# Tying each DMA of the weight sums to the matmuls of the weight unit in front of it, with descriptors of 4 KB

## The chip, the cores and the metric

The kernel runs on one core of a Trainium2 chip. The metric is the device time of one execution in microseconds. A core has a matrix engine (PE), a vector engine (DVE), an activation engine (ACT), a general engine (POOL, GpSimd) and SyncE (SP), each with its own queue of instructions that it works through in order, and 16 DMA engines that serve the DMAs issued by SP, ACT and POOL alike. Engines wait for one another through semaphores.

## The reference

The reference is the trunk of a streaming encoder: two layers over 512 frames of width 1024, in float32. What matters here is the shape of the work and the hidden layer at the end of a layer:

```python
for i in range(DEPTH):                      # 2 layers
    h = rmsnorm(x, norm1_g[i])
    z = h @ w_in[i] + b_in[i]               # 1024 x 12296: all projections
    ...                                     # branch A: mLSTM, 4 heads; branch B: retention, 4 heads
    merged = sigmoid(gm) * (y_m @ w_bm[i]) + sigmoid(gr) * (y_r @ w_br[i])
    x = x + merged @ w_out[i]
    h2 = rmsnorm(x, norm2_g[i])
    x = x + square(relu(h2 @ w_ff1[i] + b_ff1[i])) @ w_ff2[i] + b_ff2[i]
    h3 = rmsnorm(x, norm3_g[i])
    x = x + sigmoid(h3 @ w_pe_gate[i]) * (p[i] @ w_pe[i])
return rmsnorm(x, final_g)
```

## The kernel before

**Weights.** Every product is made of three matmuls (`mm3`: high part by high part, high by low, low by high), since a float32 operand is split into two parts for PE. The weights come in units of 512 KB from a stream in DRAM. SP loads them into five raw buffers (`fill_raws`, L278); ACT makes the high part (`wh`, L238) and DVE the low part (`wl`, L239) in `split`. There are three buffers of split pieces, and the split runs two pieces ahead of the matmuls (`LOOK`). Most units are a `T8`: 1024 rows by 128 columns, 24 matmuls of 512 columns. A `V` unit is a quarter of a value projection, in `values`, whose matmuls are written there and don't go through `mm3`. `unit(kind)` is called at the start of each such unit, before its matmuls are written; it counts the units.

**The order of a layer** is that of `unit_list`: 187 units. Gates (`IF`, tile names l0if, l1if); the q and k of mLSTM head 0 with a convolution (l0m0z), its values (l0m0vp), two branch gates (l0bgm), then head by head the scores (l0m0s, with a decay tile l0m0D), the product with the values (l0m0a), the output gates (l0m0o) and the transposes back (l0m0ot); then the retention heads (l0r0brq and on), the merge, `w_out`, and the hidden layer (l0f), whose second product is done in `PAIR` units.

**The weight sums.** A `PAIR` works on blocks of `w_ff2` by a scheme of seven products instead of eight. It needs four sums and differences of given blocks, t1 to t4, each 1 MB: t1 = B12 + B11, t3 = B12 + B22, t2 = t1 + B22, t4 = t2 + B21, for each of the four blocks b of a layer: 16 sums a layer. They are made by DMAs alone, DRAM to DRAM, issued on POOL: a copy of the first term into the sum's tensor (L253), then a DMA that adds the second (L256). The add needs the copy landed, and the copy of t1 into t2 needs the add of t1 landed. The tensors are called s00t to s13t in the profile (layer, block). `sum_steps(i)` gives the steps of a layer, 11 for a block: eight DMAs and three that do nothing. `unit` takes the next step at every third unit (`STEP`), counted over both layers. `fill_raws` loads the sums for the `PAIR` units (L276).

**Order on the engines.** A planner orders the instructions of each engine by its own idea of when their inputs are ready. A sum's DMA has no input but given weights and earlier sums. The trace shows what that gave: on POOL the sums of both layers stand in the first 330 us, in the middle of the work of layer 0.

**What else POOL does.** The sums of squares for the norms (L422) and their power (L436), the borders of the convolution's tiles (`conv_evac`, L682), the causal mask of each decay tile (an affine select, L729, in `m_scores`), and the power in the head norms (L750 for the mLSTM, L792 for the retention). The masked decay goes to DVE (L508), which multiplies the scores by it, and then to ACT and DVE (`split` again, tile l0m0ph), both of which also make the weights' parts in the same queues.

Of the kernel before, what the change touches and what calls it, by code (L numbers as in the profile page):

```python
# [35 lines left out]
F32R = mybir.dt.float32r  # L36
AF = mybir.ActivationFunctionType
OP = mybir.AluOpType

P = 128  # L40
T = 512
# [48 lines left out]
MADE = {"t1": ("B12", "B11"), "t3": ("B12", "B22"), "t2": ("t1", "B22"), "t4": ("t2", "B21")}  # L90
# [3 lines left out]
STEP = 3  # L94
# [95 lines left out]
def build(ctx, tc, ins, out):  # L190
    nc = tc.nc
    ve, ac, gp, te = nc.vector, nc.scalar, nc.gpsimd, nc.tensor
# [17 lines left out]
    cur = {}  # L210
# [20 lines left out]
    def ps(name):  # L231
        return psum.tile([P, T], F32, name=name, tag="ps")
# [4 lines left out]
    def split(src, hi_ap, lo_ap):  # L237
        ac.activation(hi_ap, src, AF.Copy)  # L238
        ve.tensor_sub(lo_ap, src, hi_ap.bitcast(F32))  # L239


    sums = {(i, b, x): tc.dram_tile([4, P, Q], F32, name=f"s{i}{b}{x}") for i in range(L) for b in range(4) for x in MADE}

    def block(i, b, x):
        return ins["wpairs"][i, b, GIVEN.index(x)] if x in GIVEN else sums[i, b, x]

    def flat(a):
        return a.rearrange("a p q -> (a p q)").rearrange("(r w) -> r w", r=P)

    def sum_steps(i):  # L250

        def copy(b, x):
            gp.dma_start(flat(block(i, b, x)), flat(block(i, b, MADE[x][0])))  # L253

        def add(b, x):
            gp.dma_start(flat(block(i, b, x)), flat(block(i, b, MADE[x][1])), accum_op=OP.add, max_dma_last_dim=8192)  # L256

        for b in range(4):
            for f, x in ((copy, "t1"), (copy, "t3"), (add, "t1"), (add, "t3"), (copy, "t2"), (None, None), (add, "t2"),
                         (None, None), (copy, "t4"), (None, None), (add, "t4")):  # L260
                yield (lambda f=f, b=b, x=x: f and f(b, x))


    order = [(n, x) for n, u in enumerate(units) for x in (PIECE if u[0] == "PAIR" else (0,))]
# [28 lines left out]
    def ready(k):  # L293
        while at["prep"] < min(len(order), k + 1):
            prep_next()

    def unit(kind):
        n = at["unit"]
        at["unit"] += 1
        if n % STEP == 0:  # L300
            next(cur["steps"], lambda: None)()
        assert units[n][0] == kind, (units[n], kind)
        ready(place[n, 0] + LOOK)
        return units[n], *pieces.pop((n, 0))

    def mm3(o, sh, sl, mh, ml, first, last):
        te.matmul(o, sh, mh, start=first, stop=False)  # L307
        te.matmul(o, sh, ml, start=False, stop=False)  # L308
        te.matmul(o, sl, mh, start=False, stop=last)  # L309

    def t8(act, name):

        _, wh, wl = unit("T8")
        o = ps(name)
        for k in range(KT):
            s = slice(k * P, (k + 1) * P)
            mm3(o, wh[:, s], wl[:, s], act[0][k], act[1][k], k == 0, k == KT - 1)
        return o
# [49 lines left out]
    def pair_operand(name, st, hi, lo):  # L368

        v = st.rearrange("p (q t) -> p q t", t=S)  # L370
        ve.tensor_tensor(v[:, 4:6, :], v[:, 1:3, :], v[:, 0:1, :].to_broadcast([P, 2, S]), OP.subtract)
        ve.scalar_tensor_tensor(v[:, 6, :], v[:, 5, :], -1.0, v[:, 1, :], OP.mult, OP.subtract)
        ve.scalar_tensor_tensor(v[:, 7, :], v[:, 6, :], -1.0, v[:, 3, :], OP.mult, OP.subtract)
        split(st[:, 4 * S:8 * S], hi[:, 3 * S:7 * S], lo[:, 3 * S:7 * S])
# [5 lines left out]
    class Norm:  # L380
# [18 lines left out]
        def operand(self, k, x):  # L399
            hi, lo = self.act[0][k], self.act[1][k]  # L400
            ac.activation(hi, x, AF.Copy, scale=self.col(k))
            ve.scalar_tensor_tensor(lo, x, self.col(k), hi.bitcast(F32), OP.mult, OP.subtract)

        def square(self, k, x, pool=False):
# [6 lines left out]
            if pool:  # L411
                gp.tensor_tensor(sq, x, x, OP.mult)
            else:
# [60 lines left out]
    def values(i, nm, act, nrm, bv_ap, n_):  # L474
        bvt = cur["br"].tile([P, T], F32, name=f"{nm}bv", tag="bv")
        nc.sync.dma_start(bvt, bv_ap)
        o = [ps(f"{nm}vp{j}") for j in range(NT)]
        for u in range(4):
            _, wh, wl = unit("V")
            for kk in range(2):  # L480
                k = 2 * u + kk
                s = slice(kk * T, (kk + 1) * T)
                for j in range(NT):
                    js = slice(j * P, (j + 1) * P)
                    te.matmul(o[j], act[0][k][:, js], wh[:, s], start=(k == 0), stop=False)
                    te.matmul(o[j], act[0][k][:, js], wl[:, s], start=False, stop=False)
                    te.matmul(o[j], act[1][k][:, js], wh[:, s], start=False, stop=(k == KT - 1))
        vh = [cur["low"].tile([P, 576], F32R, name=f"{nm}vh{j}", tag="vh", bufs=NT) for j in range(NT)]
        vl = [cur["low"].tile([P, 576], F32R, name=f"{nm}vl{j}", tag="vl", bufs=NT) for j in range(NT)]
        for j in range(NT):  # L490
            rows_split_v(i, None, nm, n_, j, o[j], nrm.c, bvt, vh[j], vl[j])
        return vh, vl

    def scores(nm, qh, ql, kh, kl, decay):

        ph = cur["br"].tile([P, 1280], F32R, name=f"{nm}ph", tag="ph")
        pl = cur["br"].tile([P, 1280], F32R, name=f"{nm}pl", tag="pl")
        off = 0
        offs = []
        for i in range(NT):  # L500
            w = T - i * P
            c0 = min(i * P, 256)
            o = ps(f"{nm}s{i}")
            s = slice(i * P, (i + 1) * P)
            for d in range(2):
                mm3(o[:, c0:T], kh[d][:, s], kl[d][:, s], qh[d][:, c0:T], ql[d][:, c0:T], d == 0, d == 1)
            p = tmp(f"{nm}p{i}")
            ve.tensor_tensor(p[:, :w], o[:, i * P:T], decay(i), OP.mult)  # L508
            split(p[:, :w], ph[:, off:off + w], pl[:, off:off + w])
            offs.append(off)  # L510
            off += w
        return ph, pl, offs

    def attend(nm, pt, vh, vl, c0, n, num):
        ph, pl, offs = pt
        for j in range(NT):
            o = ps(f"{nm}a{j}")
            for i in range(j + 1):
                s = slice(offs[i] + (j - i) * P, offs[i] + (j - i + 1) * P)
                mm3(o[:, :n], ph[:, s], pl[:, s], vh[i][:, c0:c0 + n], vl[i][:, c0:c0 + n], i == 0, i == j)  # L520
            ac.activation(num[:, j, :], o[:, :n], AF.Copy)
# [99 lines left out]
    x = bpool.tile([P, KT, T], F32, name="x0", tag="big")  # L621
# [15 lines left out]

    for i in range(L):
        cur["steps"] = sum_steps(i)
        act_side, ph_side = ("right", "left") if i == 0 else ("left", "right")  # L640
        xa = n1.act
# [24 lines left out]


        _, wh, wl = unit("IF")
        og = ps(f"l{i}if")
        for k in range(KT):  # L670
# [151 lines left out]
        for d in range(4):  # L822
            o = t8(xa, f"l{i}m0z{d}")
# [39 lines left out]
        for c in range(KT):  # L863
            o = t8(ym, f"l{i}bm{c}")
# [16 lines left out]
        for c in range(KT):  # L881
            o = t8(yr, f"l{i}br0{c}")
# [9 lines left out]
        mh, ml = [], []  # L892
        for c in range(KT):
# [3 lines left out]
            o = t8(yr, f"l{i}br1{c}")  # L897
# [13 lines left out]
        x = bpool.tile([P, KT, T], F32, name=f"l{i}x", tag="big")  # L911
        n2_pool = phase(f"n2{i}", act_side)
        n2 = Norm(f"l{i}n2", i, "g2", acts(n2_pool, f"l{i}n2"))
        for c in range(KT):
            xr = tmp(f"l{i}xr{c}")
            nc.scalar.dma_start(xr[:, :T], x_src[c])
            o = t8((mh, ml), f"l{i}wo{c}")
# [99 lines left out]
        for u in range(2):  # L1017
            _, wh, wl = unit("PE")
            for c in range(4):
                o = ps(f"l{i}pe{u}{c}")  # L1020
# [10 lines left out]
        last = i == L - 1  # L1031
# [21 lines left out]
        for c in range(KT - LAST if last else KT):  # L1053
            o = t8(n3.act, f"l{i}pg{c}")
# [27 lines left out]
    for a, n in enumerate(nn):  # L1082
        for c in range(KT - LAST, KT):
            _, wh, wl = ws[c - KT + LAST]
            o = ps(f"pl{a}{c}")[:, :256]
# [131 lines left out]
```

## Time and profile before

| what | value |
|---|---|
| time, median of 3 runs (lowest to highest) | 2515.81 us (2515.69 to 2518.84) |
| time of the profiled execution | 2519.82 us |
| its span, first to last instruction | 2518.1 us |
| mean granted PE clock | 0.974 |
| PE busy | 2409.3 us, 96% |
| DVE, ACT, POOL busy | 1502.3, 1051.1, 166.1 us |
| moved by DMA | 333.72 MB, of it 67.11 MB by POOL's queue (q0) |

The profile is of one execution. Busy times add up instructions; a waiting engine isn't busy. The page cuts the span into 40 slices of 63 us and gives the busy share of each in tenths. Other views give the busy time in chosen windows, the waits (who waited, at which line, for whom, how long in total, how often, and the longest), the chain of waits that ended last, the instructions of a tile or line (with least, middle and most ns, and the first and last start in us), and for DMAs the time from issue to landing.

### The profile page before, as it was taken

How to read it: one execution, taken by the hardware profiler on the slowest of the kernel's cores; microseconds unless marked ns; L12 is line 12 of the kernel's file. 1: busy time of each engine (PE TensorE's matmuls, PEld its weight loads, DVE VectorE, ACT ScalarE, POOL GpSimd, SP SyncE). 2: the span in 40 equal slices, each digit the busy share in tenths (PEclk: the TensorE clock that was granted, in tenths of full speed). 3: DMA queues.
4: the chain of work that ended last, by engine and by line, in shares of the span. 5: the costliest groups of instructions: out<-in, count | busy, mean ns of one | idle time of the engine just before them, and what ended most of it. 6: DMA issues, size and time to landing. Idle time of an engine off the chain costs nothing.

```text
span 2518.1 us, 31039 instructions
## 1 busy us (share of the span) xinstructions
PE 2409.3 (96%) x12212; PEld 2052.5 (82%) x12212; DVE 1502.3 (60%) x2276; ACT 1051.1 (42%) x1434; POOL 166.1 (7%) x266
## 2 busy tenths in 40 slices
PE   7858779999999999999999999999999999999997
PEld 5747668888888889889988888888888888988996
DVE  3655355566545557666777865565644555776675
ACT  3443342233333345544645654233323334455453
POOL 3121100000000010000020100000000001000011
PEclk7979889999999999999999999999999999999998
DMA  9999943222333344344442222222332333543441
GB/s 306 279 262 293 257 119 99 94 84 92 105 105 101 118 133 141 116 150 147 140 146 91 84 88 80 96 89 84 101 111 90 113 121 122 155 124 125 150 155 34
DMA packets 103106, 333.72 MB, mean 133 GB/s; under 512 B 11688, under 2 KB 14120, under 8 KB 98352
## 3 DMA queue, kind: packets, MB, share of 16 engines
q1 hardware_dynamic: 87392, 246.66, 30.1%
q0 software_dynamic: 5632, 67.11, 10.1%
q10 hardware_dynamic: 9936, 17.96, 2.3%
q8 instruction: 96, 1.57, 0.3%
q14 instruction: 50, 0.41, 0.1%
HBM read 323.30 MB, written 75.50 MB: 158 GB/s over the span
## 4 chain that ended last, share of the span: by engine, by line
PE 86%; DMA 10%; issue 3%; POOL 1%; DVE 1%; ACT 0%; SPq 0%; POOLq 0%; DVEq 0%; ACTq 0%
PE l1f L307 2%; PE l0f L307 2%; PE l0f L309 2%; PE l1f L309 2%; PE l0f L308 2%; PE l1f L308 2%; PE l1br L309 1%; PE l0br L309 1%; PE l0br L307 1%; PE l1br L308 1%; PE l1br L307 1%; PE l0br L308 1%; DMA s12t<-wpairs 1%; DMA s01t<-wpairs 1%; DMA s11t<-wpairs 1%
## 5 line engine op out<-in xcount | busy, mean ns | idle before, releaser
L238 ACT ACTIVATE wh<-wr 128x1024 fp32r<-128x1024 f32 x342 | 361.5, 1058 | 825.3 <-issue 161.4
L239 DVE TENSOR_TENSOR wl<-wr,wh 128x1024 fp32r<-128x1024 f32 x342 | 418.8, 1226 | 222.8 <-ACT wh L238 222.3
L307 PE MATMUL l0f<-l0n2h,wh 128*128 128x512 f32 x256 | 99.8, 390 | 0.0
L307 PE MATMUL l1f<-l1n2h,wh 128*128 128x512 f32 x256 | 99.8, 390 | 0.0
L309 PE MATMUL l0f<-l0n2h,wl 128*128 128x512 f32 x256 | 99.7, 390 | 0.0
L309 PE MATMUL l1f<-l1n2h,wl 128*128 128x512 f32 x256 | 99.7, 390 | 0.0
L308 PE MATMUL l0f<-l0n2l,wh 128*128 128x512 f32 x256 | 99.7, 389 | 0.0
L308 PE MATMUL l1f<-l1n2l,wh 128*128 128x512 f32 x256 | 99.7, 389 | 0.0
L238 ACT ACTIVATE wh_C<-wr 128x1024 fp32r<-128x1024 f32 x32 | 33.9, 1061 | 67.7 <-PE l1f L308 5.6
L309 PEld LDWEIGHTS l1f<-l1n2h,wl 128*128 128x128 f32 x256 | 48.1, 188 | 10.1
L309 PEld LDWEIGHTS l0f<-l0n2h,wl 128*128 128x128 f32 x256 | 48.1, 188 | 10.1
L308 PEld LDWEIGHTS l0f<-l0n2l,wh 128*128 128x128 f32 x256 | 48.1, 188 | 9.8
L308 PEld LDWEIGHTS l1f<-l1n2l,wh 128*128 128x128 f32 x256 | 48.1, 188 | 9.8
L307 PEld LDWEIGHTS l0f<-l0n2h,wh 128*128 128x128 f32 x256 | 48.1, 188 | 9.7
L307 PEld LDWEIGHTS l1f<-l1n2h,wh 128*128 128x128 f32 x256 | 48.1, 188 | 9.7
L239 DVE TENSOR_TENSOR wl_C<-wr,wh_C 128x1024 fp32r<-128x1024 f32 x32 | 39.2, 1226 | 18.2 <-ACT wh_C L238 17.9
L239 DVE TENSOR_TENSOR wl_A<-wr,wh_A 128x1024 fp32r<-128x1024 f32 x32 | 40.5, 1266 | 10.3 <-ACT wh_A L238 9.4
L238 ACT ACTIVATE wh_A<-wr 128x1024 fp32r<-128x1024 f32 x32 | 33.8, 1056 | 30.6 <-PE l1f L308 9.8
L238 ACT ACTIVATE wh_B<-wr 128x1024 fp32r<-128x1024 f32 x32 | 33.7, 1053 | 27.3 <-PE l0o01a L350 1.8
L239 DVE TENSOR_TENSOR wl_B<-wr,wh_B 128x1024 fp32r<-128x1024 f32 x32 | 39.1, 1222 | 7.9 <-ACT wh_B L238 7.9
L238 ACT ACTIVATE wh_D<-wr 128x512 fp32r<-128x512 f32 x32 | 20.1, 629 | 37.4 <-PE l0o01a L350 1.8
L309 PE MATMUL l0bgm<-l0n1h,wl 128*128 128x512 f32 x64 | 26.3, 411 | 7.3 <-DVE wl L239 7.3
(3709 smaller groups left out, 7578.0 us busy)
## 6 DMA issues: line engine op xcount, KB each, us to landing
wr<-wstream SPq DMA_DIRECT2D x342, 512.0 KB, 3.3
wr<-wpairs SPq DMA_DIRECT2D x96, 256.0 KB, 2.7
s00t<-wpairs POOLq DMA_DIRECT2D x4, 1024.0 KB, 11.3
s01t<-wpairs POOLq DMA_DIRECT2D x4, 1024.0 KB, 11.1
s02t<-wpairs POOLq DMA_DIRECT2D x4, 1024.0 KB, 12.2
s03t<-wpairs POOLq DMA_DIRECT2D x4, 1024.0 KB, 11.6
s10t<-wpairs POOLq DMA_DIRECT2D x4, 1024.0 KB, 11.4
s11t<-wpairs POOLq DMA_DIRECT2D x4, 1024.0 KB, 11.9
```

The lines of the kernel that those rows point to most:

```text
L238: ac.activation(hi_ap, src, AF.Copy)
L239: ve.tensor_sub(lo_ap, src, hi_ap.bitcast(F32))
L307: te.matmul(o, sh, mh, start=first, stop=False)
L308: te.matmul(o, sh, ml, start=False, stop=False)
L309: te.matmul(o, sl, mh, start=False, stop=last)
```

## The change

Each DMA of the sums gets a dependency on the last matmul that `mm3` has written when its step is taken. A step is taken at the start of every third unit, so that is as a rule the last matmul of the unit in front. In a value projection, whose matmuls don't go through `mm3`, it is an older one. The wait is a real one, on a semaphore. The step at unit 0, where no matmul has been written yet, is left for unit 3. Copies and adds get descriptors of at most 4096 bytes; before, the adds had 8192 and the copies the default.

```diff
+SYNC = mybir.DependencyInfo(mybir.DependencyClass.Sync, mybir.DependencyReason.DATA)
...
         def copy(b, x):
-            gp.dma_start(flat(block(i, b, x)), flat(block(i, b, MADE[x][0])))
+            return gp.dma_start(flat(block(i, b, x)), flat(block(i, b, MADE[x][0])), max_dma_last_dim=4096)
 
         def add(b, x):
-            gp.dma_start(flat(block(i, b, x)), flat(block(i, b, MADE[x][1])), accum_op=OP.add, max_dma_last_dim=8192)
+            return gp.dma_start(flat(block(i, b, x)), flat(block(i, b, MADE[x][1])), accum_op=OP.add,
+                                max_dma_last_dim=4096)
+
+        def step(f, b, x):
+
+            if f:
+                tc.add_manual_dep(f(b, x).ins, cur["mm"].ins.name, SYNC, reason="pace of the sums")
...
-                yield (lambda f=f, b=b, x=x: f and f(b, x))
+                yield lambda f=f, b=b, x=x: step(f, b, x)
...
-        if n % STEP == 0:
+        if n % STEP == 0 and "mm" in cur:
             next(cur["steps"], lambda: None)()
...
         te.matmul(o, sh, ml, start=False, stop=False)
-        te.matmul(o, sl, mh, start=False, stop=last)
+        cur["mm"] = te.matmul(o, sl, mh, start=False, stop=last)
```

## The prediction

> **What bounds the kernel now.** I read the page first.
>
> ```profile
> PE 2409.3 (96%) x12212; PEld 2052.5 (82%) x12212; DVE 1502.3 (60%) x2276; ACT 1051.1 (42%) x1434; POOL 166.1 (7%) x266
> PEclk7979889999999999999999999999999999999998
> DMA  9999943222333344344442222222332333543441
> ```
>
> PE is the bound, but the slices show one place where it isn't: the first five or six (63 us each) have gaps in the granted clock and DMA engines busy all the time. Afterwards both are quiet. So I cut the span by stage (the view of busy time by windows; columns: window, its length, busy us of PE, PEld, DVE, ACT, POOL with instruction counts, granted clock, DMA share, GB/s). The cuts are the first matmul of the first value product and of the first retention projection in each layer:
>
> ```profile
> L485 PE MATMUL l0m0vp<-wh,l0n1h x32: 389/389/390, 63.7 to 84.8; 128*128 128x512 f32 x32
> L307 PE MATMUL l0r0brq<-l0n1h,wh x16: 388/389/475, 387.0 to 397.3; 128*128 128x512 f32 x16
> L485 PE MATMUL l1m0vp<-wh,l1n1h x32: 389/389/390, 1338.7 to 1359.8; 128*128 128x512 f32 x32
> L307 PE MATMUL l1r0brq<-l1n1h,wh x16: 388/390/478, 1572.6 to 1583.0; 128*128 128x512 f32 x16
> ```
> ```profile
> 24.00:63.70 39.70, 26.89 (x108) 21.56 (x107) 14.95 (x24) 10.36 (x16) 16.88 (x30) 0.79 1.01 299
> 63.70:387.00 323.30, 251.44 (x1135) 206.46 (x1134) 168.57 (x310) 131.61 (x209) 54.64 (x104) 0.87 0.84 238
> 387.00:1309.70 922.70, 921.20 (x4768) 790.58 (x4767) 560.33 (x788) 375.20 (x479) 33.31 (x23) 1.00 0.37 117
> 1309.70:1338.70 29.00, 28.98 (x131) 23.60 (x130) 16.20 (x28) 10.42 (x13) 3.55 (x16) 1.00 0.42 137
> 1338.70:1572.60 233.90, 233.90 (x1134) 196.29 (x1134) 170.12 (x311) 133.03 (x211) 17.61 (x46) 1.00 0.26 85
> ```
>
> The second and the fifth row are the same mLSTM stage, of layer 0 and of layer 1: 1135 and 1134 matmuls, about 310 DVE instructions each. Layer 0 takes 323.3 us, layer 1 takes 233.9 with PE never idle. The difference, 89.4 us, has this form in PE's waits of the layer 0 window (layer 1's list is empty):
>
> ```profile
> PE l0m0ot L539 <- DVE l0m0num L533: 18.3, 1, 18.3
> PE l0m2ot L539 <- DVE l0m2num L533: 17.3, 1, 17.3
> PE l0m3k1z L307 <- ACT wh L238: 13.4, 1, 13.4
> PE l0m1o L309 <- DVE wl L239: 8.3, 1, 8.3
> PE l0bgm L309 <- DVE wl L239: 7.3, 1, 7.3
> PE l0m1k1z L307 <- ACT wh L238: 6.8, 1, 6.8
> PE l0m1k1z L309 <- DVE wl L239: 0.4, 1, 0.4
> ```
>
> They sum to 71.8 us. The remaining 17.5 us is PE busy time (251.4 against 233.9): the matmuls after each gap run at a lower granted clock. What stands behind these waits is in the chain of waits of 60 to 330 us, DVE's waits, two instructions of the mask that m_scores applies, and the last sums' adds (ns of issue least, middle, most; first and last start):
>
> ```profile
> by line: issue 18.6%; DMA s12t<-wpairs 8.1%; DMA s01t<-wpairs 8.0%; DMA s11t<-wpairs 7.9%; DMA s10t<-wpairs 7.6%; DMA s13t<-wpairs 6.8%; DMA s03t<-s03t 6.2%; DMA s02t<-s02t 6.0%; DMA s01t<-s01t 5.5%; DMA s11t<-s11t 5.5%; DMA s12t<-s12t 5.4%
> DVE l0m0p L508 <- POOL l0m0D L729: 18.8, 3, 16.6
> L724 ACT ACTIVATE l0m0D<-l0m0D x4: 293/294/311, 113.2 to 140.7; 128x128 f32<-128x128 f32 x4
> 132.92 0.31 POOL L729 TENSOR_SCALAR_AFFINE_SELECT l0m0D<-l0m0D 128x128 f32<-128x128 f32 x1
> L256 POOL DMA_DIRECT2D s13t<-wpairs x4: 823/828/1097, 285.4 to 325.7; - x4
> ```
>
> ACT had the first decay tile ready at 113.5; POOL masked it at 132.9. POOL is 7% busy: it stood in its own queue, where every sum of the layer waits for the landing of the sum before it (copy, then add, then the copy of that). The sums of both layers, 64 in all, are in it: the last add of layer 1 is issued at 325.7. The masked tile goes to DVE and from there to ACT's split, and ACT's splits of weights queue behind that one: so PE ends up waiting for "wh". **POOL's queue, blocked by DMA landings, is the bound of the first 330 us.**
>
> **The change, part by part.**
>
> *Each sum waits for a matmul (64 sums; 88 steps, 24 of them empty).* A sum can no longer be issued before the weight unit in front of its step has run. Three units lie between steps. A unit is 24 matmuls; the l0m0vp row has 32 of each kind (96 matmuls, four units) in about 21.8 us, so a unit is 5.4 us and steps are 16.3 us or more apart. What a sum depends on was issued two steps, 33 us, earlier (the t4 and t2 adds too, by the empty steps; a little less where steps fall into value units, which set no new matmul). The landings (copies, then adds):
>
> ```profile
> DMA to landing us min/median/max: 5.2/12.6/17.3
> DMA to landing us min/median/max: 7.7/11.5/18.0
> q0 software_dynamic: 4876, 56.65, 67.1%
> wr<-wstream SPq DMA_DIRECT2D x36, 512.0 KB, 10.7
> wr<-wstream SPq DMA_DIRECT2D x36, 512.0 KB, 3.3
> L276 SPq DMA_DIRECT2D wr<-s03t x16: 319/423/1827, 1187.1 to 1243.8; - x16
> ```
>
> Even the longest, 18.0 us on saturated engines, is over before the dependent sum comes up. So POOL's waits for landings go, and with them the 89.4 us: layer 0's stage should take layer 1's 233.9.
>
> What the new wait blocks: POOL stands until PE has finished the unit in front. Behind it in POOL's queue are the masks, the conv borders (L682), the hv powers (L750, L792) and the norm sums (L422). Nearly all feed from matmuls at or after that unit, so the wait costs them at most the issue. An add's issue took 0.83 us in the middle and 1.10 at most (the s13t row above). Descriptors of 4 KB make 256 parts of a 1 MB sum where the adds' 8 KB made 128. No row has this size; I bound the issue by 0.8 (no growth) and 2.2 us (growth of the longest in step with the parts) and take 1.2, near the row's longest, since it is the same operation on the same bytes. Its tightest cover is the power of m0 in layer 1:
>
> ```profile
> L533 DVE TENSOR_SCALAR l1m0num<-l1m0num,l1m0mv,l1m0hv x4: 408/409/415, 1408.9 to 1409.9; 128x256 f32<-128x256 f32 x4
> L539 PE MATMUL l1m0ot<-ident,l1m0num x8: 269/272/273, 1413.6 to 1414.3; 128*128 128x128 f32 x8
> ```
>
> The scaling is done at 1410.3, PE wants it at 1413.6: 3.3 us of cover, more than 1.2 or 2.2. I take the cost as nothing; without that cover it is the issue itself, up to 2.2 us a time.
>
> *The layer 1 sums move by a layer*, past everything POOL does in layer 0 after 326 us, into layer 1, which was undisturbed. There and in layer 0 they share the DMA engines with the weights. In the mLSTM window of layer 0 the sums' queue moved 56.65 MB (the q0 row: packets, MB, share) in 67.1% of 323.3 us, so one sum takes 4.0 us of all 16 engines; one in 16.3 us is 25%, on top of the 0.26 that the layer 1 row shows: about half busy. The two wr rows are weights' landing in layer 0's and layer 1's mLSTM window: even at 10.7 us on full engines no PE wait names a load. Cost: nothing; covered by the five buffers in front. SP's loads of the sums come late enough: the first of s03t is at 1187.1, in the last of the four blocks of pairs, while its last step stands at the fourth tile of the hidden layer, ahead of the first block.
>
> *The start.* The first sum moves from 1.4 us behind the second conv unit, so the loads of x have the engines alone, and the norm's adds on POOL aren't stopped by landings.
>
> ```profile
> 21.03 0.72 ACT L401 ACTIVATE l0n1h<-x,bc 128x512 fp32r<-128x512 f32 x1 [0.27 <-DMA x<-xT]
> 23.90 0.44 PE L307 MATMUL l0m0z<-l0n1h,wh 128*128 128x512 f32 x1
> 25.92 3.74 ACT L414 ACTIVATE l0n1sq<-x 128x512 f32<-128x512 f32 x7
> 43.53 0.83 POOL L256 DMA_DIRECT2D s00t<-wpairs  x1 [8.01 <-DMA s00t<-s00t]
> L422 POOL TENSOR_TENSOR l0n1sum<-l0n1sum,l0n1sq x6: 1303/1542/2004, 26.6 to 45.9; 128x512 f32<-128x512 f32 x6
> 48.15 1.87 PE L429 MATMUL l0n1ss<-ones,l0n1sum 128*128 128x2 f32 x8 [12.70 <-DVE l0n1sum L420]
> q1 hardware_dynamic: 2772, 6.62, 57.9%
> q0 software_dynamic: 208, 3.15, 33.6%
> ```
>
> The q rows are of the first 30 us: loads got 57.9% of the engines, sums 33.6%. With the sums' part, the last piece of x, in use at 21.0, comes at about 2 + 19 x 57.9 / 91.5 = 14.0. The conv tiles then start 2.9 us later (as 23.90 after 21.03), at 16.9. The squares start 4.9 us after 14.0 (25.92 after 21.03), at 18.9; the adds 0.7 later, six at 1.54 us, to 28.9; DVE's last add 0.7 and the step to PE 0.7: l0n1ss at 30.3. PE is through two tiles at 16.9 + 10.9 = 27.8, so it waits 2.5 us (12.7 before). Layer 1's row of 29.0 us, less its 5.4 us unit of gates, gives 23.6 for the same four tiles and the norm. The value product starts at 16.9 + 23.6 + 2.5 = 43.0 in place of 63.7: 20.7 us less. Ends: x at 10 with no wait gives 36.5 (27 less); the first sum queued ahead of the norm's adds, which then start at PE's 27.8 + 1.2, gives about 52 (12 less).
>
> **The sum.** 89.4 + 20.7 = 110.1. The 922.7 us to layer 1 and all of layer 1 run on a PE that is never idle and stay. The profiled execution took 2519.82 for its span of 2518.1; the median of the runs, 2515.81, is 4.0 lower, and I take the gain off the median: **2515.8 - 110.1 = 2405.7.** Its own range goes by the ends of the start, 2399 (27 less) to 2414 (12 less).
>
> **Rivals.**
> *A, POOL's issues come through (0.18).* If the masks and powers are late by each issue, and the 20 sums whose steps fall into the two mLSTM stages (ten a layer) each cost PE one issue of 1.2 us, 24 us come back: 2430; with a start at 52 as well, 2439. For it: ACT's splits stand in order behind the mask's chain. Against it: 3.3 us of cover at the tightest place.
> The Trainium skill, "SBUF — State Buffer", section "SBUF: two separate sides", has a rule that speaks for A: GpSimd writes the descriptors of its own DMAs through a port pair it shares with VectorE, and some VectorE instructions lock it out for their whole length. By that rule an issue would stand until such a DVE instruction ends; the longest issue in the s13t row is 1.10 us, so the trace doesn't show it at a size that counts.
>
> *B, a loop of POOL and PE (0.05, slower).* A sum waits for PE's unit N, a mask queued behind it is due sooner, ACT's split of the weights for unit N+2 waits behind the mask's, and PE stalls on its own wait. The price of such a stall, clock included, is that of before: 89.4 over seven waits, 12.8 us. Against 110.1 us gained it decides from nine stalls on; if 12 of the 20 sums did so the time would be 2405.7 + 153.6 = 2559. A few stalls, two to eight, give 2431 to 2508 (0.07). Against it: the order of POOL's queue follows the order in which work comes up, and a mask's matmuls precede the unit.
>
> *C, the sums still block (0.03).* If 4 KB adds land later than the 33 us that the pace leaves, POOL waits for landings again and the time stays near 2516. Against it: 18.0 us at worst, on full engines.
>
> **Chances.** Forecast 0.67, A 0.18, a few stalls 0.07, B 0.05, C 0.03. A measurement of this kernel can tell about 0.2% (5 us) from no change. Faster 0.92, same 0.03, slower 0.05. The range for 8 in 10 goes from the forecast's low end, 2399, to A's end, 2439, and a little wider since the runs before spread over 3 us: 2397 to 2440.
>
> **What would show it.** Right: the window from the first value product to the first retention projection is about 234 us in both layers with clock 1.00; POOL's waits before sums name PE, none a landing of s-tiles; l0m0vp starts near 43; DMA share near 0.5 through most of both layers until the hidden layer. Wrong: PE waits on wh or num in either mLSTM window (A or B, told apart by their length, about 1 us or near 10), or POOL waiting for s-tiles (C). What would make the forecast wrong at a stroke is a POOL queue in which the sums stand ahead of masks that are due earlier.

## The result and the profile after

| | before | after |
|---|---|---|
| median of 4 runs (lowest to highest) | 2516.81 us (2515.69 to 2518.84) | 2403.72 us (2402.4 to 2404.6) |
| span of the profiled execution | 2518.1 us | 2402.8 us |
| mean granted PE clock | 0.974 | 0.996 |
| PE busy | 2409.3 us | 2381.9 us |

The changed kernel is faster: the ratio of the times is 0.9549, with a 95% interval of 0.9533 to 0.9566. That is 113.1 us between the medians, against 110.1 us forecast. The predicted 2405.7 us is 2.0 us off.

The first lines of the page of the changed kernel, the ones that showed the gap before (busy tenths and granted clock in 40 slices, now of 60 us):

```profile
PE   9999999999999999999999999999999999999997
PEclk9999999999999999999999999999999999999998
DMA  6433453545365553444444445344454654443451
q0 software_dynamic: 17408, 67.11, 11.8%
```

The gaps of the first slices are gone, and with them the full DMA engines. The sums' queue (q0) moves the same 67.11 MB in three times as many packets, 17408 against 5632 on the page of before, and takes 11.8% of a shorter span. The same cuts as before, at the first matmul of the first value product, of the first retention projection, and of layer 1's gates (window, length, then busy us and instruction counts of PE, PEld, DVE, ACT, POOL, granted clock, DMA share, GB/s):

```profile
40.20:274.10 233.90, 233.90 (x1135) 196.26 (x1134) 170.40 (x310) 132.56 (x209) 28.77 (x55) 1.00 0.42 125
274.10:1196.00 921.90, 920.16 (x4768) 789.38 (x4767) 559.10 (x788) 375.27 (x478) 51.04 (x45) 1.00 0.47 142
1196.00:2402.80 1206.80, 1189.86 (x6145) 1018.73 (x6143) 749.25 (x1147) 524.20 (x721) 83.02 (x126) 0.99 0.44 135
1225.10:1459.00 233.90, 233.90 (x1135) 196.25 (x1135) 170.11 (x310) 133.07 (x211) 25.44 (x56) 1.00 0.42 125
```

The mLSTM stage of layer 0 takes 233.9 us with PE never idle, to the tenth what layer 1 took before and takes now. So the account of the span is: start 63.7 to 40.2, 23.5 us less; stage 323.3 to 233.9, 89.4 us less; the rest of layer 0 922.7 to 921.9, and layer 1 1208.4 to 1206.8, together 2.4 us less. The sum is 115.3 us, the difference of the two spans. It is 2.2 us more than the difference of the medians, since the profiled execution of before was 3.0 us above its median and that of after 0.8 us.

POOL's instructions around the first masks (start, us, engine, line, operation; in brackets how long POOL stood before it, and for whom):

```profile
79.86 0.29 POOL L736 TENSOR_SCALAR_AFFINE_SELECT l0m0D<-l0m0D 128x128 f32<-128x128 f32 x1 [9.69 <-ACT l0m0D L731]
82.40 0.63 POOL L736 TENSOR_SCALAR_AFFINE_SELECT l0m0D<-l0m0D 128x128 f32<-128x128 f32 x1 [2.25 <-ACT l0m0D L731]
84.72 0.93 POOL L257 DMA_DIRECT2D s00t<-wpairs  x1 [1.69 <-PE l0m1q0z L316]
85.96 0.73 POOL L736 TENSOR_SCALAR_AFFINE_SELECT l0m0D<-l0m0D 128x128 f32<-128x128 f32 x1 [0.32 <-ACT l0m0D L731]
```

The masks now wait for ACT, which makes the decay tile, and no longer for a sum. One add stands between two masks; it waits 1.7 us for its matmul and takes 0.9 us, and POOL is still ready for the next mask 0.3 us before ACT hands over its input.

### The profile page after: what moved, and what is told of

Its sections match the earlier page's. It is cut to its first block, busy times and chain, and to the rows that moved or that the text cites. A ratio compares the mean times of both kernels' runs of the same rounds, so it can differ in the third digit from the quotient of the medians.

```text
span 2402.8 us, 31079 instructions
## 1 busy us (share of the span) xinstructions
PE 2381.9 (99%) x12212; PEld 2036.4 (85%) x12212; DVE 1500.7 (62%) x2276; ACT 1051.8 (44%) x1434; POOL 178.9 (7%) x266
## 3 DMA queue, kind: packets, MB, share of 16 engines
q0 software_dynamic: 17408, 67.11, 11.8%
## 4 chain that ended last, share of the span: by engine, by line
PE 97%; DVE 1%; issue 1%; DMA 1%; POOL 0%; ACT 0%; SPq 0%; POOLq 0%; DVEq 0%; ACTq 0%
PE l0f L314 2%; PE l1f L314 2%; PE l1f L316 2%; PE l1f L315 2%; PE l0f L316 2%; PE l0f L315 2%; PE l1br L315 1%; PE l1br L314 1%; PE l0br L314 1%; PE l0br L316 1%; PE l0br L315 1%; PE l1br L316 1%; PE l0bgm L314 1%; PE l1bgm L314 1%; PE l0pg L314 1%; PE l0pg L315 1%
## 5 line engine op out<-in xcount | busy, mean ns | idle before, releaser
L240 DVE TENSOR_TENSOR wl_C<-wr,wh_C 128x1024 fp32r<-128x1024 f32 x32 | 39.2, 1226 | 18.3 <-ACT wh_C L239 17.9
L429 POOL TENSOR_TENSOR l1n3sum<-l1n3sum,l1n3sq 128x512 f32<-128x512 f32 x6 | 8.2, 1360 | 331.3 <-ACT l1n3sum L421 306.8
```

The lines of the kernel that those rows point to most:

```text
L429: gp.tensor_tensor(self.sum, self.sum, sq, OP.add)
```

## The experiments

The theory: POOL works its queue in order, sums that wait for landings stood ahead of masks, conv borders and norm powers that were due, and these held up DVE, ACT and with them PE. The rivals: the full DMA engines held up the weights; the large descriptors did; or it is the wait itself, which thins out the traffic.

### The parts of the change

*The changed kernel again, on the same chip as its parts* (r1).

> The changed kernel itself, beside its parts on the same chip: 2404 us (2402 to 2406), about 113 us under the kernel before. Both theories expect this.

Measured: 2404.27 us (2402.9 to 2405.68), ratio 0.9557 (0.9544 to 0.957).

*The waits alone* (r2): descriptors as before.

```diff
-            return gp.dma_start(..., max_dma_last_dim=4096)
+            return gp.dma_start(...)
-                                max_dma_last_dim=4096)
+                                max_dma_last_dim=8192)
```

> The waits alone; copies and adds keep the descriptors of before. Theory (POOL's queue, blocked by landings, was the bound): all of the gain, within 4 us of the changed kernel, 2400 to 2408, and 233.9 us for the mLSTM stage of layer 0. Rival (large descriptors hold up the weights' loads): weights land later than 3.3 us in the middle, PE waits for wh, 2415 or more.

Measured: 2403.85 us (2403.28 to 2406.52), ratio 0.9558 (0.9544 to 0.9571). All of the gain is there without the 4 KB descriptors. The rival of large descriptors falls.

*The descriptors alone* (r4): no dependency on a matmul.

```diff
             if f:
-                tc.add_manual_dep(f(b, x).ins, cur["mm"].ins.name, SYNC, reason="pace of the sums")
+                f(b, x)
```

> Descriptors of 4 KB alone, no waits; the first step is at unit 3 in the program, but nothing holds it there. Theory: POOL is blocked by landings as before, 2516 with at most 15 us to either side. Rival (large descriptors hold up the weights): most of the gain, 2450 or less.

Measured: 2528.69 us (2527.74 to 2533.24), ratio 1.0055 (1.0042 to 1.0069): slower than before by half a per cent. From its windows and waits:

```profile
67.20:400.60 333.40, 252.37 (x1134) 206.73 (x1133) 168.56 (x310) 131.62 (x209) 57.12 (x104) 0.86 0.86 230
PE l0m3k1z L314 <- ACT wh L239: 18.7, 1, 18.7
PE l0m0ot L546 <- DVE l0m0num L540: 18.5, 1, 18.5
PE l0m2ot L546 <- DVE l0m2num L540: 18.2, 1, 18.2
```
```profile
DMA to landing us min/median/max: 7.7/12.7/21.0
```

It is the picture of before, a little worse: the stage takes 333.4 us (323.3), its start is at 67.2 (63.7), and the adds, whose landings the last row shows, take 12.7 us in the middle and 21.0 at most (11.5 and 18.0). So where POOL waits for landings the smaller descriptors seem to cost something, and where it doesn't they cost nothing (r1 against r2). The first is not shown cleanly: r4 also takes its first step at unit 3 and not at unit 0, and four of POOL's instructions stand at another place than before.

### Order or wait?

*The order alone* (r3). The dependency is kept for the planner but makes no semaphore.

```diff
-SYNC = mybir.DependencyInfo(mybir.DependencyClass.Sync, mybir.DependencyReason.DATA)
+SYNC = mybir.DependencyInfo(mybir.DependencyClass.NoSync, mybir.DependencyReason.DATA)
```

> The same dependencies for the planner, which then puts POOL's queue in almost the same order, but no semaphore: a sum may run as soon as POOL comes to it. Theory: what counts is what stands behind a landing in POOL's queue, so the order alone brings 100 us or more of the 113 (2402 to 2416). Rival (the waits matter because they thin out the traffic): the sums run together wherever POOL is idle, the DMA engines are full again and most of the gain goes, 2450 or more.

Measured: 2404.52 us (2402.02 to 2405.59), ratio 0.9557 (0.9544 to 0.957): all of the gain, with no sum waiting for a matmul. By the order of their starts in the two traces, POOL's instructions are those of the changed kernel but for the place of one memset (5 of ACT's and 13 of DVE's stand elsewhere, none of PE's). The sums among POOL's instructions from 226 to 283 us, with four instructions of other kinds left out:

```profile
226.23 1.03 POOL L257 DMA_DIRECT2D s00t<-wpairs  x1
233.75 0.60 POOL L254 DMA_DIRECT2D s01t<-wpairs  x1
249.22 0.62 POOL L254 DMA_DIRECT2D s01t<-wpairs  x1
249.84 0.98 POOL L257 DMA_DIRECT2D s01t<-wpairs  x1
255.28 0.91 POOL L257 DMA_DIRECT2D s01t<-wpairs  x1 [4.47 <-DMA s01t<-wpairs]
261.78 0.57 POOL L254 DMA_DIRECT2D s01t<-s01t  x1 [5.59 <-DMA s01t<-wpairs]
272.10 0.87 POOL L257 DMA_DIRECT2D s01t<-wpairs  x1 [9.75 <-DMA s01t<-s01t]
282.10 0.58 POOL L254 DMA_DIRECT2D s01t<-s01t  x1 [9.13 <-DMA s01t<-wpairs]
```

The sums do run together and POOL does stand for their landings again, 4 to 10 us at a time. It costs nothing: PE waits for nothing in this stretch. What the change does is to move the sums in POOL's queue; the semaphore that comes with it isn't needed for the time. The rival is not tested by this run alone, since in the mLSTM stage the DMA share stays at 0.45 (0.42 in the changed kernel); the next run fills the engines.

### Traffic without landings, landings without traffic

*Traffic* (r5): the changed kernel with 36 copies more in the stage, whose landing nobody waits for.

```diff
+PER = 1
...
+    junk = [tc.dram_tile([4, P, Q], F32, name=f"j{k}") for k in range(72)]
+
+    def more(n):
+
+        if 5 <= n < 41:
+            for k in range(PER):
+                d = gp.dma_start(flat(junk[at["junk"]]), flat(ins["wpairs"][1, at["junk"] % 4, k % 4]), max_dma_last_dim=4096)
+                tc.add_manual_dep(d.ins, cur["mm"].ins.name, SYNC, reason="flood")
+                at["junk"] += 1
...
+        more(n)
         assert units[n][0] == kind, (units[n], kind)
```

> The changed kernel with 36 more copies of 1 MB, DRAM to DRAM, that nothing reads: one at the start of each of the units 5 to 40 of layer 0, with the same wait for the matmul in front. They fill the DMA engines in the mLSTM stage of layer 0 as the sums did before, but no instruction of POOL waits for their landing. Theory (landings in POOL's queue): the stage stays at 234 us with at most 6 more, the whole at 2404 to 2412, though the weights land as late as before (10 us). Rival (full DMA engines were the cause): the stage goes towards 323, the whole to 2450 or more.

Measured: 2405.11 us (2404.2 to 2406.84), ratio 0.9559 (0.9543 to 0.9575). The stage's window and the weights' landing in it:

```profile
40.10:274.00 233.90, 233.90 (x1136) 196.27 (x1134) 170.25 (x311) 135.70 (x211) 48.76 (x91) 1.00 0.87 283
wr<-wstream SPq DMA_DIRECT2D x36, 512.0 KB, 7.0
```

The DMA engines are as full as before (share 0.87 against 0.84, 283 GB/s against 238), the weights land in 7.0 us and not in 3.3, and the stage is still 233.9 us. Full DMA engines by themselves weren't the cause. (The weights' landing before was 10.7 us, which this run doesn't reach.)

*Landings* (r9): the changed kernel with eight small DMAs, each waiting for the one before, ahead of the first mask of each head of layer 0. They start when ACT has the tile ready.

```diff
-                ac.activation(d[:, 0:P], d[:, 0:P], AF.Exp)
+                e = ac.activation(d[:, 0:P], d[:, 0:P], AF.Exp)
...
+                if a == 0 and i == 0:
+                    for k in range(LINKS):
+                        z = gp.dma_start(link[h][k + 1], link[h][k] if k else ins["ident"][:, 0:32])
+                        if k == 0:
+                            tc.add_manual_dep(z.ins, e.ins.name, SYNC, reason="start of the links")
-                gp.affine_select(d[:, 0:P], ...)
+                m = gp.affine_select(d[:, 0:P], ...)
+                if a == 0 and i == 0:
+                    tc.add_manual_dep(m.ins, z.ins.name, ORDER, reason="mask behind the links")
```

> The changed kernel with eight small DMAs (16 KB each) ahead of the first mask of each of the four heads of layer 0, on POOL: the first starts when ACT has the decay tile ready, each next one waits for the landing of the one before, and the mask stands behind the last. No traffic to speak of, but landings ahead of masks, as before. Theory: masks are about 20 us late; some 10 us are covered by the two weight units split ahead, so each head costs PE about 10 us and a little clock: 2430 to 2470, with PE waits on wh or num. Rival (without full DMA engines a late mask is covered): 2402 to 2410.

Measured: 2447.41 us (2444.29 to 2448.84), ratio 0.9728 (0.9711 to 0.9744), 43 us over the changed kernel. The first links of head 0, its first mask, the stage's window and PE's waits in it:

```profile
78.39 0.56 POOL L741 DMA_DIRECT2D k<-ident  x1 [9.91 <-ACT l0m0D L734]
80.64 0.50 POOL L741 DMA_DIRECT2D k<-k  x1 [1.69 <-DMA k<-ident]
...
101.83 0.49 POOL L741 DMA_DIRECT2D k<-k  x1 [1.70 <-DMA k<-k]
102.32 0.31 POOL L744 TENSOR_SCALAR_AFFINE_SELECT l0m0D<-l0m0D 128x128 f32<-128x128 f32 x1
```
```profile
38.60:315.90 277.30, 247.44 (x1136) 204.68 (x1134) 168.89 (x311) 135.01 (x211) 43.86 (x87) 0.93 0.36 108
PE l0m3a L317 <- ACT l0m3ph L241: 8.4, 1, 8.4
PE l0m0ot L549 <- DVE l0m0num L543: 8.1, 1, 8.1
PE l0m2ot L549 <- DVE l0m2num L543: 7.5, 1, 7.5
PE l0m0a L317 <- ACT l0m0ph L241: 5.1, 1, 5.1
```

The first mask of head 0 is 23.9 us late (102.3 after 78.4). DMA is idle most of the time (0.36), and yet the stage is 43.4 us longer: about 30 us of PE waits (29.1 in the four rows) and 13.5 us of busy time (247.44 against 233.90), the mark of a lower granted clock (0.93). So landings in POOL's queue cost PE time without full DMA engines. But this is about half of the 89.4 us, and not by the same waits. The waits were expected on wh or num; two are on num, and the others are on the split of the masked scores (ph), none on wh. The two on num (m0ot, m2ot) carry the names of rows of the list before, but here the power on POOL that they need comes at once when DVE asks for it (for head 0 at 127.6 us), and so they follow from the late masks; before, they stood behind other work of POOL, as the section on the prediction shows.

### The start

*One wait only* (r6): of all sums only the first waits for a matmul.

```diff
             if f:
-                tc.add_manual_dep(f(b, x).ins, cur["mm"].ins.name, SYNC, reason="pace of the sums")
+                d = f(b, x)
+                if "held" not in cur:
+                    cur["held"] = True
+                    tc.add_manual_dep(d.ins, cur["mm"].ins.name, SYNC, reason="pace of the sums")
```

> Only the first sum waits for its matmul (4 KB descriptors for all); the others follow freely. It keeps the loads of x and the first norm free of sums and leaves the mLSTM stage blocked. Theory: the start is regained (l0m0vp at about 40 and not 67), the stage stays near 330 us, so 2529 less 24 = 2505 (2495 to 2515). Rival (the start sets the stage's order too): most of the gain, under 2450.

Measured: 2528.93 us (2524.04 to 2529.42), ratio 1.0045 (1.003 to 1.006). Both expectations missed, for a plain reason:

```profile
1.39 0.78 POOL L254 DMA_DIRECT2D s00t<-wpairs  x1 [0.34 <-issue]
11.77 1.34 POOL L254 DMA_DIRECT2D s01t<-wpairs  x1
```

The planner put another copy of block 0 at 1.39 us and the sums of block 1 behind it, so the start wasn't free, and l0m0vp came at 63.8. The stage stayed near 330 us as the theory had it (333.0 us), so it is only the start that failed to come. The run says only that one wait isn't enough.

*All sums behind one early matmul* (r8), the same question put right.

```diff
-                tc.add_manual_dep(f(b, x).ins, cur["mm"].ins.name, SYNC, reason="pace of the sums")
+                cur.setdefault("first", cur["mm"])
+                tc.add_manual_dep(f(b, x).ins, cur["first"].ins.name, SYNC, reason="pace of the sums")
```

> All 64 sums wait for one and the same matmul, the last of the second convolution tile (about 25 us), and follow freely behind it. The start is without sums, the mLSTM stage of layer 0 is blocked as before. Theory: l0m0vp at about 40 to 44 and not 67, the stage at about 323 to 335: 2495 to 2515. Rival (what counts is only that the first microseconds are free): under 2450.

Measured: 2500.85 us (2499.33 to 2506.35), ratio 0.9942 (0.9927 to 0.9957). The stage's window and DVE's waits:

```profile
38.90:369.50 330.60, 254.06 (x1136) 208.39 (x1134) 167.91 (x311) 134.41 (x211) 58.50 (x107) 0.86 0.96 258
DVE l0m2p L516 <- POOL l0m2D L737: 37.1, 3, 28.9
DVE l0m0p L516 <- POOL l0m0D L737: 23.8, 3, 17.0
```

The start is as early as in the changed kernel (38.9), the stage is blocked as with 4 KB descriptors and no wait (330.6 against 333.4), and 27.8 us are gained against r4, whose start was at 67.2. The two terms of the sum are separate: the start can be had without the stage.

### A closer pace

*A step at every unit* (r7): `STEP = 1` in place of 3.

> The changed kernel with a step at every unit (STEP = 1) and not at every third: a sum comes 10.9 us after what it depends on and not 33, and all sums of a layer fall into its mLSTM stage. Theory: adds land in 9 to 13 us, so POOL waits for some landings, a few us each, in both layers' mLSTM stages: 2406 to 2440. Rival (any pace cures it, as the wait is what counts): 2402 to 2406.

Measured: 2406.85 us (2404.13 to 2407.7), ratio 0.9563 (0.9548 to 0.9577), at the low end of the theory's range and 0.9 us above the rival's. POOL's waits have landings in them again:

```profile
POOL s10t L254 <- DMA s10t<-wpairs: 14.9, 2, 9.6
POOL s03t L257 <- DMA s03t<-s03t: 11.4, 1, 11.4
POOL s12t L257 <- DMA s12t<-wpairs: 9.4, 2, 6.1
POOL s00t L254 <- DMA s00t<-wpairs: 9.2, 1, 9.2
```

The stage took 234.0 us nonetheless, with the DMA share at 0.71. The 2.6 us over r1 are within the spread of the runs (2.8 us for r1, 3.6 for r7); the profiled start is a little late (l0m0vp at 41.6, against 38.6 in r1 and 40.2 in the first profile of the changed kernel). So a few landings of up to 11 us, between work placed where the planner expects the sums, are covered; I had expected some of them to reach PE.

No variant was faster than the changed kernel by more than the runs spread; r1, r2 and r3 are the same within 1 us.

## Why the prediction was right

**What bounds the kernel.** That POOL's queue, blocked by landings, is the bound holds: with the sums moved in it the stage takes 233.9 us, with semaphores or without (r1, r3), traffic without landings costs nothing (r5), and with landings put ahead of masks 43 us are lost with the DMA engines idle most of the time (r9). The way from there to PE is only in part the one that the prediction followed. It followed the late masks to ACT's splits. DVE's waits for POOL before, in the mLSTM stage of layer 0, show that masks, powers and conv borders were late alike:

```profile
DVE l0m2p L508 <- POOL l0m2D L729: 26.0, 3, 25.2
DVE l0m1hv L751 <- POOL l0m1hv L750: 15.4, 1, 15.4
DVE l0m0hv L751 <- POOL l0m0hv L750: 13.9, 1, 13.9
DVE l0m3k0cv L688 <- POOL l0m3k0zp L682: 11.1, 1, 11.1
DVE l0m02cv L688 <- POOL l0m02zp L682: 8.2, 1, 8.2
```

Put beside PE's seven waits by their times, the late masks of heads 0 and 2 stand in front of those at l0m1k1z and l0m3k1z, 20.6 of the 71.8 us. The longest, l0m0ot (18.3 us), stands behind the power of head 0: DVE had handed over the power's input by 160.4 us, and POOL came to it at 174.6, behind sums. The power of head 1 stands in front of l0m1o (8.3), a conv border in front of l0bgm (7.3), and another border and then the power of head 2 in front of l0m2ot (17.3). So 51.2 of the 71.8 us stand behind powers and borders. The prediction names them as work behind the sums, but its account of the waits before has only the masks; that they are late is read from the trace, and no run delays them alone.

**The stage, 89.4 us.** Measured 89.4. The reading of two layers' same stage against each other gave the size without any model of the single stalls, so the size didn't suffer from the incomplete account of them.

**The start, 20.7 us.** Measured 23.5. The mis-sized terms can be read in ACT's and POOL's instructions of the changed kernel:

```profile
6.10 5.32 ACT L408 ACTIVATE l0n1h<-x,bc 128x512 fp32r<-128x512 f32 x8
16.26 3.25 POOL L429 TENSOR_TENSOR l0n1sum<-l0n1sum,l0n1sq 128x512 f32<-128x512 f32 x2 [7.41 <-ACT l0n1sq L421]
24.15 1.27 POOL L429 TENSOR_TENSOR l0n1sum<-l0n1sum,l0n1sq 128x512 f32<-128x512 f32 x1
```

ACT goes through all eight pieces of x in one run of 5.3 us and is at the last at about 10.7 us; the sharing of the engines by their shares had given 14.0. Four of the norm's six adds take 1.3 us and not 1.54, with no sum issued between them. What remained of PE's wait for the norm was 1.1 us, against 2.5. A third term went the other way: from the first conv tile (13.8 us, forecast 16.9) to the value product (40.2) PE took 25.3 us besides that wait, at a granted clock of 0.94, where 23.6 had been taken from layer 1 at 1.00. So the miss of 2.8 us is 3.1 and 1.4 less 1.7: in part the errors cancelled by luck. One execution doesn't give the start more closely than this either: in r1, the same kernel, the value product starts at 38.6.

**What was costed at nothing.** The issue of an add took 0.87 to 1.00 us with 4 KB descriptors against the 1.2 taken; no mask or power came through to PE, so rival A did not occur. Nor does any issue show, at a size that counts, the lock of which the Trainium skill ("SBUF — State Buffer", section "SBUF: two separate sides") speaks for some DVE instructions: no issue of a sum in the changed kernel is above 1.0 us. The rest of the kernel, costed at nothing, gained 2.4 us; the runs don't tell why.

**Rivals B and C.** B's loop of POOL and PE did not form: the longest of POOL's waits for a matmul and the landings of the adds, in the changed kernel, were these:

```profile
POOL s01t L254 <- PE l0r1brk L316: 41.1, 1, 41.1
```
```profile
DMA to landing us min/median/max: 7.9/9.3/12.9
```

POOL stood for 41 us, but nothing that PE came to wait for stood behind it. C did not occur: 12.9 us at most, against the 33 us that the pace leaves as a rule. One landing was waited for all the same, by an add of s02t, for 4.8 us: the trace puts it down to a copy issued only 5.5 us earlier, so the pace doesn't leave 33 us everywhere, and the sign "none a landing of s-tiles" failed once, at no cost to PE.

**What the prediction had only in part.** It gave the semaphore a part in the cure: "a sum can no longer be issued before the weight unit in front of its step has run". The runs show that the planner's order is enough without it (r3). That B and C hang on the planner's order was in its last sentence, but it had no run to tell order from wait.

**Open.** With the sums moved, the planner also ordered some instructions of ACT and DVE anew: by the order of their starts in the traces, 25 of ACT's 1434 and 54 of DVE's 2276 stand at another place, none of PE's and none of SP's DMAs. No run has the new order of ACT and DVE with the old one of POOL. Two runs speak against it as the cause: r5 differs from the changed kernel in 23 of ACT's and 39 of DVE's instructions and keeps the 233.9 us, and r8 differs from before in 12 and 41 and keeps the blocked stage. In r9 the planner moved more, 54 of ACT's, 79 of DVE's and 17 of PE's instructions, so how much of its 43 us is the late masks alone is not shown. Why the planner set the sums so early is not tried either.

## What to carry to other kernels

A DMA that waits for another's landing holds up everything behind it in the queue of the engine that issues it (here up to 15.3 us at a time), even where that engine is busy 7% of the time: look at who stands behind it before looking at bandwidth, and follow each kind of work there to the engine that waits for it, not the first kind alone. If a planner orders the queues, a dependency on a far-off instruction can place such DMAs where nothing behind them is due; here the order was enough. Where the same stage runs twice, once disturbed and once not, the difference of the two windows is what there is to gain, whatever the single stalls are.

## What was not expected of the hardware

With the engines at 0.87 of their time and weights landing in 7.0 us, a PE-bound stage of 234 us did not lengthen at all (r5). With smaller descriptors the landing of an add took a little longer, by 1.2 us in the middle on full engines (12.7 in r4, 11.5 before; the copies, 12.5 and 12.6, didn't), and by 0.5 us at the changed kernel's pace (9.3, and 8.8 with 8 KB in r2):

```profile
DMA to landing us min/median/max: 7.7/8.8/11.7
```

That row is r2's.
